# Six banks for an output projection, and a reordered start and end of the down products, in a fused decoder layer

## The chip, the cores and the metric

One core of a Trainium2 chip runs the whole layer as one program. The metric is the device time of one execution in microseconds. TensorE is called PE, VectorE DVE, ScalarE ACT, GpSimd POOL, and SyncE SP; SP issues most of the DMA transfers and POOL issues the stores of results.

## The reference

One inference step of a decoder layer (D = 1024) for a prompt of 1024 rows and a sample group of 64 rows (8 sequences of 8), which share the weights. The part that matters here is the end of the layer:

```python
    x = x + merged @ w_out
    f, conv_state = conv_ffn(rmsnorm(x, norm2_g), conv_prefix.astype(x.dtype), w_ffn_gate, w_ffn_up,
                             ffn_conv_w, ffn_conv_b, w_ffn_down)
    x = x + f
```

`conv_ffn` computes g = h @ w_gate and u = h @ w_up (1024 x 2816 each), a causal convolution of width 3 over the rows of g, then (gelu(gc) * u) @ w_down (2816 x 1024). After the layer comes a last `rmsnorm` of x with `final_norm_g`: each row is divided by the root of its mean square and multiplied by a gain per column.

## The kernel before

Everything is float32. A matmul runs on operands of a reduced format, so each operand is split into a high part (ACT casts it, L113) and a low part (DVE subtracts the high part from the source, L114), and a product is three matmuls: high x high, high x low and low x high. A matmul is 128 x 128 by 128 x 512; its result lies in one PSUM bank of 128 x 512.

The program is written in an order of its own, but a planner sets the order of the instructions on each engine: it takes the text's order as a priority, estimates durations, and puts an instruction ahead where its inputs and its buffer are free earlier. On the chip each engine and each DMA queue then works strictly in that order. Tiles with one tag turn through a fixed number of buffers.

The three places:

*Output projection (L944 to L1006).* For the two halves `nb` of 512 columns of `w_out`, the weights are loaded and split; then one product for the sample's rows and one for each of the eight row tiles t of the prompt (24 matmuls, L191). Each goes to a PSUM bank `nat`, of which there are two. `add_sq` (L928) adds the bank to x on DVE, in place, and squares the sum on ACT, writing the squares into the bank and their sum to `ssn`. In the second half x1 is stored to DRAM by a POOL DMA (L978), then normalised in place (`norm2`, L934 to L938: sum, a chain of small instructions for the reciprocal root at L120 to L126, one multiply over 1024 columns), transposed and split into the blocks B11, B21, B22 and T1 to T4 for the FFN products, which are computed by Winograd's scheme of seven products in place of eight. PSUM also has two tiles `big` of two banks each, which this stage doesn't use. The raw weights of the first two FFN blocks (L918) are loaded to buffers with the tag `raw`, of which there are four.

*FFN products (L1132).* Forty-four weight blocks, seven products each. The change does not touch their text.

*Down products (L1166 to L1481).* The product with `w_down` is also computed by Winograd's scheme, in seven passes in the order P1, P2, P5, P6, P7, P3, P4, each of 11 steps k. A step is twelve matmuls (four row tiles t, three each, L1298) to four banks of a ring of seven with tag `b`; P2 goes on adding into P1's banks and P7 into P6's. In P2, P6, P7 and P3 two more matmuls per step compute the sample's rows in a bank `sb` (L1338). `prep_down` loads and splits the operands of a step, four steps ahead of the matmuls, into five buffers `hd`. The first four operands come through `raw` buffers, the other seven of P1 through the tiles XB and ST, whose memory becomes free only after the FFN products. `sum1` and `sum2` turn ST into the sums that P5 and P6 use. After four steps the sample's own operand is made (L1390 to L1412): two transposes on PE, a multiply on DVE, casts on ACT and subtractions on DVE, and then the run goes on with step 4.

`evac` empties the banks after the last step of a pass: after P1 and P6 all four at once, after the others tile 0 at once and one more per step. Rows' squares are summed by `sq` (L1250), whose junk output goes to the bank just read. `norm` (L1252 to L1264) is the final norm: for row tiles 0 to 3 and the sample ACT multiplies by the reciprocal root (L1262), POOL by the gain (L1263) and POOL issues the store (L1264); for row tiles 4 to 7, which are finished at the end of P4, DVE does both in one instruction per half (L1259) and SP issues the stores. P4's last four steps are held back and computed tile by tile, so that the row tiles are finished one after another.

Of the kernel before, what the change touches and what calls it, by code (L numbers as in the profile page):

```python
# [16 lines left out]
P = 128  # L17
# [15 lines left out]
def hybrid_step(ctx, tc, x_prompt, x_sample, mem_prompt, cache_k, cache_v, page_table, state_pool,  # L33
# [888 lines left out]
    with tc.tile_pool(name="p5", bufs=1, reuse_waits="tile") as p5:  # L922
# [11 lines left out]
        def norm2(xt, n, t):  # L934
# [3 lines left out]
            nc.vector.scalar_tensor_tensor(xt, xt, r, g2b[:n], op0=ALU.mult, op1=ALU.mult)  # L938
# [14 lines left out]
        for nb in range(2):  # L953
            n0 = nb * 512
            wf = load_w(cols(w_out, n0))
            if nb == 0:
                nc.sync.dma_start(x1s, x_sample)
                for t in range(NT):
                    nc.sync.dma_start(x1[t], x_prompt[t * P:(t + 1) * P])
            else:  # L960
                nc.sync.dma_start(g2b, bc(norm2_g[0], P))
                raws[0], raws[1] = raw_ffn(0), raw_ffn(1)
            pt = nat()
# [8 lines left out]
            for i, t in enumerate((0, 2, 1, 3, 4, 6, 5, 7) if nb else range(NT)):  # L972
                pt = nat()
                mm_n(pt, wf, macts, t)
                add_sq(x1[t], (pt,), pt, P, t, nb)
                if nb == 0:
                    continue
                nc.gpsimd.dma_start(x1_d[t], x1[t])  # L978
                norm2(x1[t], P, t)
                if i == 3:  # L980
                    T1, T2 = [ap_.tile([P, 2, 4, 512], F32R, tag="act", bufs=4, name=f"T{q}") for q in (1, 2)]
                a = t // 2
                if t % 2 == 0:
                    put(B11, x1[t][:, 0:512], a)
                    put(B21, x1[t][:, 512:D], a)
                    continue
                xa, xb = x1[t - 1], x1[t]
                put(B22, xb[:, 512:D], a)
                nc.vector.tensor_tensor(xa[:, 0:512], xb[:, 0:512], xa[:, 0:512], op=ALU.subtract)
                nc.gpsimd.tensor_tensor(xb[:, 0:512], xb[:, 512:D], xb[:, 0:512], op=ALU.subtract)  # L990
                nc.vector.tensor_tensor(xb[:, 512:D], xb[:, 512:D], xa[:, 0:512], op=ALU.subtract)
                nc.gpsimd.tensor_tensor(xa[:, 512:D], xa[:, 512:D], xb[:, 512:D], op=ALU.subtract)
                todo.append((xa, xb, a))
                if T1 is not None:
                    for (xa, xb, a) in todo:
                        put(T1, xa[:, 0:512], a)
                        put(T2, xb[:, 512:D], a)
                        late.append((xa, xb, a))
                    todo = []
# [9 lines left out]
    with tc.tile_pool(name="fa", bufs=1, reuse_waits="tile") as fa:  # L1009
# [220 lines left out]
        def sum1(k):  # L1230
            ld(ST[k][:, 0], fA(1, 1, k))
            if k < 4:
# [4 lines left out]
        def sum2(k):  # L1237
            if k < 4:
# [9 lines left out]
        def sq(x, junk, i, c):  # L1248
            n = x.shape[0]
            nc.scalar.activation(junk, x, AF.Square, accum_out=ssf[:n, i, c:c + 1])  # L1250

        def norm(x, i, dst, late):  # L1252
            n = x.shape[0]
            ss = sm.tile([P, 1], F32, tag="ss", name=f"ss{uid()}")[:n]
            tt(ss, ssf[:n, i, 0:1], ssf[:n, i, 1:2], ALU.add)
            r = rstd_of(ss, n, 1.0 / D, 1)
            if late:
                for c in (LO, HI):
                    nc.vector.scalar_tensor_tensor(x[:, c], x[:, c], r, gfb[:n, c], op0=ALU.mult, op1=ALU.mult)  # L1259
                    nc.sync.dma_start(dst[:, c], x[:, c])  # L1260
            else:
                nc.scalar.activation(x, x, AF.Identity, scale=r)  # L1262
                nc.gpsimd.tensor_tensor(x, x, gfb[:n], op=ALU.mult)  # L1263
                nc.gpsimd.dma_start(dst, x)  # L1264

        def smp2(c, op):
            for h in range(2):
                tt(ys[:, c], ys[:, c], sb[0][h * TS:(h + 1) * TS], op)

        def evac(p, t, b):  # L1270
            y0, y1 = Y[t], Y[t + 4]
            if p == "P1":
                nc.scalar.copy(U[t], b)
            elif p == "P2":
                tt(y0[:, LO], y0[:, LO], b, ALU.add)
                sq(y0[:, LO], b, t, 0)
            elif p == "P5":
                tt(y0[:, HI], b, U[t], ALU.subtract)
                nc.scalar.copy(y1[:, HI], b)
            elif p == "P6":  # L1280
                tt(y0[:, HI], y0[:, HI], b, ALU.subtract)
            elif p == "P7":
                tt(U[t], U[t], b, ALU.add)
                tt(y1[:, HI], y1[:, HI], U[t], ALU.subtract)
                sq(y1[:, HI], b, t + 4, 1)
                tt(y1[:, LO], y1[:, LO], U[t], ALU.add)
            elif p == "P3":
                tt(y0[:, HI], y0[:, HI], b, ALU.add)
                sq(y0[:, HI], b, t, 1)
                norm(y0, t, y_prompt[t * P:(t + 1) * P], False)  # L1290
            else:
                tt(y1[:, LO], y1[:, LO], b, ALU.add)
                sq(y1[:, LO], b, t + 4, 0)
                norm(y1, t + 4, y_prompt[(t + 4) * P:(t + 5) * P], True)
# [6 lines left out]

        def run_steps(s0, s1):
            for g in range(4, s0 + 4 if s0 else 0):
                prep_down(g)
            for s in range(s0, s1):
# [3 lines left out]
                if s >= 4:  # L1309
# [13 lines left out]
                    if pend:  # L1323
                        evac(*pend.pop(0))
# [17 lines left out]
                now = 4 if p in ("P1", "P6") else 1  # L1342
                for t in range(4):
                    if t < now:
                        evac(p, t, banks[t])
                    else:
                        pend.append((p, t, banks[t]))
                if p == "P6":
                    smp2(LO, ALU.add)
                if p == "P7":  # L1350
                    smp2(LO, ALU.subtract)
                    smp2(HI, ALU.add)
                    sq(ys[:, LO], sb[0][0:TS], NT, 0)
                if p == "P3":
                    smp2(HI, ALU.add)
                    sq(ys[:, HI], sb[0][0:TS], NT, 1)
                    norm(ys, NT, y_sample, False)
            if s1 == len(steps):
                for t in range(4):
                    for (k, h) in held:  # L1360
                        mm4("P4", k, t, h)
                    evac("P4", t, banks[t])
# [27 lines left out]
        run_steps(0, 4)  # L1390
# [25 lines left out]
    with tc.tile_pool(name="fb", bufs=1, reuse_waits="tile") as fb:  # L1416
        XB, ST = {}, {}
        for k in (4, 5, 6, 7, 8, 9, 10, 0, 1, 2, 3):
            XB[k] = fb.tile([P, 2, 512], F32, name=f"XB{k}")
            ST[k] = fb.tile([P, 2, 512], F32, name=f"ST{k}")  # L1420
        ssf = fb.tile([P, NT + 1, 2], F32, name="ssf")
        run_steps(4, len(steps))
# [59 lines left out]
```

## Time and profile before

| | us |
|---|---|
| median of 3 runs | 1769.6 (1768.57 to 1771.12) |
| the profiled execution | 1768.74 |
| its span from the first to the last instruction | 1767.0 |
| PE busy | 1698.4 (96%) |
| DVE busy | 952.8 (54%) |
| ACT busy | 723.2 (41%) |
| POOL busy | 412.1 (23%) |
| mean granted clock of PE, of 1 | 0.986 |

PE is busy for nearly the whole span, and the chain of waits that ended last runs on PE for 84% of it. A busy PE is not PE at its peak: a matmul takes about twice as long at the lower of the two clocks (1.2 GHz, shown as 0.50; 2.4 GHz is 1.00). So a stretch is read by its idle time and by the granted clock together.

### The profile page before, as it was taken

Reading aid. Unit: us, or ns where it says so; the run is one execution under the profiler, and the core shown is the slowest. Engines: PE = TensorE matmul, PEld = TensorE weight load, DVE = VectorE, ACT = ScalarE, POOL = GpSimd, SP = SyncE. Lnnn points to the kernel's source line nnn. Section 1 sums busy time; section 2 is a strip of 40 time slices with the busy share of each in tenths; the row PEclk is TensorE's granted clock in tenths of the full one; section 3 lists DMA queues with packets and bytes.
Section 4 is the critical chain, followed back from the end, with each engine's and each line's share of the span. In section 5 each row is a group of like instructions: output and inputs, shape, how many; then the busy total and the mean of one; then the engine's idle time right before and its main releaser. Section 6 shows DMA issues by size and latency. Waiting matters only on the chain.

```text
span 1767.0 us, 22904 instructions
## 1 busy us (share of the span) xinstructions
PE 1698.4 (96%) x8157; PEld 1327.8 (75%) x8157; DVE 952.8 (54%) x1648; ACT 723.2 (41%) x1397; POOL 412.1 (23%) x438
## 2 busy tenths in 40 slices
PE   7999999999999999999989899999999999899996
PEld 5887876765666787777768778888888888688875
DVE  6412134330220766676734776666666666578778
ACT  5422234331330766665522354444444444344343
POOL 1113020300200324202200244444444442100003
PEclk9999999999999999999999999999999999999998
DMA  7432251357665424154542132222222222891513
GB/s 272 152 131 82 79 171 59 110 180 237 201 223 193 136 86 142 34 167 155 182 167 66 72 63 72 73 73 73 73 73 72 73 73 84 299 337 49 177 68 137
DMA packets 142359, 228.18 MB, mean 129 GB/s; under 512 B 26703, under 2 KB 64109, under 8 KB 142245
## 3 DMA queue, kind: packets, MB, share of 16 engines
q1 hardware_dynamic: 126453, 178.25, 31.3%
q0 software_dynamic: 15792, 48.48, 8.1%
q8 instruction: 64, 1.05, 0.2%
q14 instruction: 50, 0.41, 0.1%
HBM read 176.19 MB, written 50.54 MB: 128 GB/s over the span
## 4 chain that ended last, share of the span: by engine, by line
PE 84%; DVE 6%; DMA 3%; issue 3%; ACT 2%; SPq 1%; POOL 1%; DVEq 0%; POOLq 0%; ACTq 0%
PE nat L182 18%; PE big L1132 17%; PE P L1298 10%; PE nat L191 8%; PE nat L1132 7%; PE big L182 4%; PE tp L110 4%; PE av L1047 3%; PE big L781 2%; PE av L811 2%; PE nat L199 2%; PE av L110 1%; PE av L571 1%; PE sb L1338 1%; PE big L675 1%
## 5 line engine op out<-in xcount | busy, mean ns | idle before, releaser
L182 PE MATMUL nat<-act,hl 128*128 128x512 f32 x1344 | 359.3, 405 | 0.0
L182 PEld LDWEIGHTS nat<-act,hl 128*128 128x128 f32 x1344 | 242.7, 189 | 62.1 <-issue 15.1
L1298 PE MATMUL P<-hd 128*128 128x512 f32 x924 | 223.7, 397 | 12.9 <-ACT hd L113 6.1
L1298 PEld LDWEIGHTS P<-hd 128*128 128x128 f32 x924 | 176.7, 192 | 52.5 <-ACT hd L113 6.7
L191 PE MATMUL nat<-hl,act 128*128 128x512 f32 x768 | 187.6, 402 | 6.8 <-ACT nat L932 5.1
L191 PEld LDWEIGHTS nat<-hl,act 128*128 128x128 f32 x768 | 146.9, 193 | 39.0 <-ACT nat L932 5.5
L1132 PE MATMUL big<-B,wA 128*128 128x512 f32 x528 | 131.2, 396 | 0.0
L114 DVE TENSOR_TENSOR hl<-raw,hl 128x1024 fp32r<-128x1024 f32 x52 | 66.4, 1288 | 117.1 <-ACT hl L113 115.8
L1132 PEld LDWEIGHTS big<-B,wA 128*128 128x128 f32 x528 | 95.9, 188 | 24.4 <-ACT gu L1157 6.3
L114 DVE TENSOR_TENSOR wB<-stm,wB 128x512 fp32r<-128x512 f32 x44 | 50.7, 1154 | 102.1 <-ACT wB L113 102.1
L474 POOL DMA_DIRECT2D gl<-ev x48 | 26.2, 547 | 280.8 <-ACT ev L473 256.5
L473 ACT COPY ev<-nat 128x512 f32<-128x512 f32 x48 | 28.1, 586 | 116.1 <-PE nat L182 115.6
L1115 POOL TENSOR_TENSOR stm<-rf,stm 128x512 f32<-128x512 f32 x22 | 28.7, 1304 | 188.3 <-DVE wB L114 188.2
L1132 PE MATMUL nat<-B,wC 128*128 128x512 f32 x264 | 70.5, 389 | 0.0
L113 ACT CAST hl<-raw 128x1024 fp32r<-128x1024 f32 x60 | 62.5, 1051 | 16.8 <-PE nat L182 7.9
L1132 PE MATMUL big<-T,wC 128*128 128x512 f32 x264 | 66.4, 400 | 0.0
L114 DVE TENSOR_TENSOR hd<-rd,hd 128x1024 fp32r<-128x1024 f32 x37 | 49.3, 1334 | 30.2 <-ACT hd L113 25.9
L1132 PE MATMUL nat<-T,wB 128*128 128x512 f32 x264 | 64.9, 394 | 0.0
L1132 PE MATMUL big<-T,wD 128*128 128x512 f32 x264 | 64.0, 391 | 0.0
L113 ACT CAST hd<-rd 128x1024 fp32r<-128x1024 f32 x37 | 38.9, 1051 | 60.1 <-PE sb L1338 31.9
L1132 PE MATMUL big<-T,wB 128*128 128x512 f32 x264 | 63.4, 389 | 0.0
L1148 DVE TENSOR_TENSOR gu<-gu,big 128x512 f32<-128x512 f32 x44 | 30.3, 688 | 57.2 <-PE big L1132 57.2
(450 smaller groups left out, 3168.8 us busy)
## 6 DMA issues: line engine op xcount, KB each, us to landing
raw<-in_w_in SPq DMA_DIRECT2D x40, 512.0 KB
kr<-in_cache_k SPq DMA_DIRECT2D x64, 256.0 KB
vr<-in_cache_v SPq DMA_DIRECT2D x64, 256.0 KB
rd<-f_d SPq DMA_DIRECT2D x59, 256.0 KB
gl<-ev POOLq DMA_DIRECT2D x48, 256.0 KB, 2.7
rd<-in_w_ffn_down SPq DMA_DIRECT2D x48, 256.0 KB
rf<-in_w_ffn_gate SPq DMA_DIRECT2D x22, 512.0 KB
rf<-in_w_ffn_up SPq DMA_DIRECT2D x22, 512.0 KB
```

The lines of the kernel that those rows point to most:

```text
L110: nc.tensor.transpose(out, in_, ident[:n, :n])
L113: nc.scalar.copy(hi, src)
L114: (lo_eng or nc.vector).tensor_tensor(lo, src, hi.bitcast(F32), op=ALU.subtract)
L182: nc.tensor.matmul(out, wf(k, pw)[:, n0:n0 + P], acts[c][ph][:, k, :], start=(k == ks[0] and (pw, ph) == (0, 0)), stop=(k == ks[-1] and (p ...
L191: nc.tensor.matmul(out, acts[c][ph][:, k, o:o + P], wf(k, pw), start=(k == ks[0] and (pw, ph) == (0, 0)), stop=(k == ks[-1] and (pw, ph) = ...
L199: nc.tensor.matmul(out, stack[:, k, :], wf(k, pw), start=(k == ks[0] and pw == 0), stop=(k == ks[-1] and pw == 1))
L781: nc.tensor.matmul(S[:, k0:k0 + n], Qd[:, m, part, qs], Kst[:, m, k0:k0 + n], start=(part == 0), stop=(part == 1))
L811: nc.tensor.matmul(av[:, :P], aT[:, k * P:(k + 1) * P], vn[:, k0 + k], start=(k0 + k == 0), stop=(k0 + k == i))
L1047: nc.tensor.matmul(pt[:, i * 256:(i + 1) * 256].rearrange("p (h x) -> p h x", h=2), xs[:, k] if k < 4 else st2[:, k - 4], w[n1][:, :, k] i ...
L1132: nc.tensor.matmul(out, wt[:, pw, k], Bt[:, ph, k], start=(start and k == 0 and (pw, ph) == (0, 0)), stop=(k == 3 and (pw, ph) == (1, 0)), ...
L1148: nc.vector.tensor_tensor(hv(g, i), hv(g, i), q(x), op=ALU.add)
L1298: nc.tensor.matmul(banks[t], h[:, ph, 0, t * P:(t + 1) * P], h[:, pw, 1], start=(k == 0 and p not in ("P2", "P7") and (pw, ph) == (0, 0)), ...
```

## The change

1. *Banks of the projection.* `obank` gives the nine products of the first half six banks: two `nat` and the four halves of the two `big` tiles. The second half keeps the two `nat`.
2. *x1 in halves.* In the first half the lower 512 columns of x1 are stored as soon as they are added. In the second half `add_sq` writes the sum to a stage (`stg`: two `raw` buffers, four halves) in place of x1; the store reads the stage, and `norm2` multiplies the two halves in two instructions. Only the first FFN block is loaded ahead; the second follows where the FFN products begin.
3. *Start of the down products.* Step 4's operand also comes through a `raw` buffer and is prepared ahead of step 0; after step 0 the sample's operand is made, and then the run goes on with step 1. XB[4] and ST[4] are filled later, by `sum1` and `sum2`.
4. *Reading the banks.* `evac` is a generator: each of its pieces is one or two instructions, and `more(n)` runs n pieces at a step. In P7 the first piece adds bank 0 into U, all squares take bank 3 for junk, and the sample's adds come between.
5. *The final norm.* The reciprocal root for row tiles 0 to 3 is one chain on four columns; DVE multiplies by root and gain in one instruction of 1024 columns per tile, also for the sample, and POOL only issues the stores. The upper halves of row tiles 4 to 7 are multiplied by the gain ahead of time. `last` takes the place of `norm` at the end of P4: one instruction of the chain fewer, the upper half scaled on ACT, the lower on DVE.

```diff
-        def add_sq(xt, pts, junk, n, t, nb):
+        def add_sq(xt, pts, junk, n, t, nb, out=None):
             xh = xt[:, nb * 512:(nb + 1) * 512]
+            out = xh if out is None else out
             for q in pts:
-                nc.vector.tensor_tensor(xh, xh, q, op=ALU.add)
-            nc.scalar.activation(junk, xh, AF.Square, accum_out=ssn[:n, t, nb:nb + 1])
+                nc.vector.tensor_tensor(out, xh, q, op=ALU.add)
+            nc.scalar.activation(junk, out, AF.Square, accum_out=ssn[:n, t, nb:nb + 1])
...
+            for (c, src) in ((slice(0, 512), xt[:, 0:512]), (slice(512, D), hi)):
+                nc.vector.scalar_tensor_tensor(xt[:, c], src, r, g2b[:n, c], op0=ALU.mult, op1=ALU.mult)
+
+        obs, obc = [], [0]
+
+        def obank(nb):
+            obc[0] += 1
+            if nb or obc[0] % 6 in (1, 2):
+                return nat()
+            if not obs:
+                pt = big()
+                obs.extend((pt[:, 0], pt[:, 1]))
+            return obs.pop(0)
...
-                raws[0], raws[1] = raw_ffn(0), raw_ffn(1)
-            pt = nat()
+                raws[0] = raw_ffn(0)
+                stg = [wp.tile([P, 2, 512], F32, tag="raw", bufs=4, name=f"stg{i}") for i in range(2)]
+            pt = obank(nb)
...
-                add_sq(x1[t], (pt,), pt, P, t, nb)
                 if nb == 0:
+                    add_sq(x1[t], (pt,), pt, P, t, nb)
+                    nc.gpsimd.dma_start(x1_d[t][:, 0:512], x1[t][:, 0:512])
                     continue
-                nc.gpsimd.dma_start(x1_d[t], x1[t])
-                norm2(x1[t], P, t)
+                hi = stg[i % 4 // 2][:, i % 2]
+                add_sq(x1[t], (pt,), pt, P, t, nb, hi)
+                nc.gpsimd.dma_start(x1_d[t][:, 512:D], hi)
+                norm2(x1[t], P, t, hi)
...
-                if k < 4:
+                if k < 5:
                     src = rawt(fA(0, 0, k), wB(0, 0, k))
...
+        def norm(xs_, i, dsts):
+            n, w = xs_[0].shape[0], len(xs_)
+            ss = sm.tile([P, w], F32, tag=f"rs_s{w}", bufs=1, name=f"ss{uid()}")[:n]
+            tt(ss, ssf[:n, 0, i:i + w], ssf[:n, 1, i:i + w], ALU.add)
+            r = rstd_of(ss, n, 1.0 / D, w)
+            for j, (x, dst) in enumerate(zip(xs_, dsts)):
+                def go(x=x, dst=dst, j=j):
+                    nc.vector.scalar_tensor_tensor(x, x, r[:, j:j + 1], gfb[:n], op0=ALU.mult, op1=ALU.mult)
+                    nc.gpsimd.dma_start(dst, x)
+                yield go
+
+        def last(t, b):
+            y, i = Y[t + 4], t + 4
+            dst = y_prompt[i * P:(i + 1) * P]
+            tt(y[:, LO], y[:, LO], b, ALU.add)
+            sq(y[:, LO], b, i, 0)
...
+            nc.vector.tensor_scalar(a, ssf[:, 0, i:i + 1], 1.0 / D, ssf[:, 1, i:i + 1], op0=ALU.mult, op1=ALU.add)
+            nc.scalar.activation(q, a, AF.Sqrt)
...
+            nc.scalar.activation(y[:, HI], y[:, HI], AF.Identity, scale=r)
+            nc.sync.dma_start(dst[:, HI], y[:, HI])
+            nc.vector.scalar_tensor_tensor(y[:, LO], y[:, LO], r, gfb[:, LO], op0=ALU.mult, op1=ALU.mult)
+            nc.sync.dma_start(dst[:, LO], y[:, LO])
...
             elif p == "P7":
-                tt(U[t], U[t], b, ALU.add)
-                tt(y1[:, HI], y1[:, HI], U[t], ALU.subtract)
-                sq(y1[:, HI], b, t + 4, 1)
-                tt(y1[:, LO], y1[:, LO], U[t], ALU.add)
+                yield lambda: tt(U[0], U[0], bk[0], A)
+                for h in range(2):
+                    yield lambda h=h: smp1(LO, S, h, sbk)
+                    yield lambda h=h: smp1(HI, A, h, sbk)
+                for t in range(1, 4):
+                    yield lambda t=t: tt(U[t], U[t], bk[t], A)
+                for t in range(4):
+                    yield lambda t=t: tt(Y[t + 4][:, HI], Y[t + 4][:, HI], U[t], S)
+                    yield lambda t=t: (sq(Y[t + 4][:, HI], bk[3], t + 4, 1), tt(Y[t + 4][:, LO], Y[t + 4][:, LO], U[t], A))
+                sq(ys[:, LO], bk[3][0:TS], NT, 0)
             elif p == "P3":
...
+                yield from norm([Y[t] for t in range(4)], 0, [y_prompt[t * P:(t + 1) * P] for t in range(4)])
+                for t in range(4):
+                    yield lambda t=t: tt(Y[t + 4][:, HI], Y[t + 4][:, HI], gfb[:, HI], ALU.mult)
+                nc.vector.tensor_scalar(ssf[:, 1, 4:8], ssf[:, 1, 4:8], 1.0 / D, EPS, op0=ALU.mult, op1=A)
+                yield from norm([ys], NT, [y_sample])
...
-                    if pend:
-                        evac(*pend.pop(0))
+                    more(4 if k == 0 else 1 if p != "P3" and p != "P4" or k > 6 else 2)
...
-        run_steps(0, 4)
+        prep_down(4)
+        run_steps(0, 1)
...
-        for k in (4, 5, 6, 7, 8, 9, 10, 0, 1, 2, 3):
+        for k in (5, 6, 7, 8, 9, 10, 0, 1, 2, 3, 4):
...
-        run_steps(4, len(steps))
+        run_steps(1, len(steps))
```

## Rows read from the trace of the kernel before

**Rows 1.** Windows of time: stretch, its length, busy us of each engine (instructions), clock, DMA share, GB/s.
```profile
897.00:949.00 52.00, 46.89 (x195) 38.20 (x194) 11.23 (x15) 9.28 (x20) 0.00 (x0) 0.93 0.34 120
1046.00:1506.00 460.00, 460.00 (x2163) 372.72 (x2162) 286.94 (x367) 197.67 (x356) 180.32 (x158) 1.00 0.24 74
1506.00:1546.00 40.00, 33.96 (x142) 26.98 (x141) 21.95 (x26) 14.91 (x24) 6.22 (x6) 0.91 0.93 316
...
1719.70:1757.70 38.00, 32.98 (x133) 25.87 (x131) 33.96 (x73) 19.23 (x34) 17.21 (x10) 0.91 0.38 132
```

**Rows 2.** Chain of waits, in P5 and P6: start, us, what.
```profile
1580.97 32.64 PE P L1298 x144
```

**Rows 3.** Timeline of the projection's start: start, us, engine, what [idle before <- releaser].
```profile
897.44 5.64 PE L191 MATMUL nat<-hl,act 128*128 128x512 f32 x24
...
905.84 1.40 DVE L931 TENSOR_TENSOR x1s<-x1s,nat 64x512 f32<-64x512 f32 x2 [5.55 <-DMA x1s<-in_x_sample]
...
908.19 41.16 PE L191 MATMUL nat<-hl,act 128*128 128x512 f32 x168 [5.11 <-ACT nat L932]
```

**Rows 4.** Groups of DVE instructions, 955 to 1033: busy us, mean ns, idle before.
```profile
L938 DVE SCALAR_TENSOR_TENSOR x<-x,rsy,g2b 128x1024 f32<-128x1024 f32 x8 | 10.3, 1285 | 3.9 <-DMA x_d<-x 3.7
...
L126 DVE TENSOR_TENSOR rsy<-rsy,rst 128x1 f32<-128x1 f32 x8 | 1.3, 160 | 0.3
```

**Rows 5.** Waits in the second half: total us, times, longest.
```profile
DVE x L938 <- DMA x_d<-x: 3.7, 4, 1.3
...
PE av L110 <- DVE x L938: 2.9, 1, 2.9
```

**Rows 6.** Timeline where the FFN products begin.
```profile
1028.70 1.69 SPq L1023 DMA_DIRECT2D cwb<-in_ffn_conv_b  x1
...
1029.42 1.14 ACT L113 CAST wA<-rf 128x512 fp32r<-128x512 f32 x2
```

**Rows 7.** Timeline of the start of the down products.
```profile
1518.33 0.34 PE L110 MATMUL sb<-ident,gs 64*128 64x64 f32 x2
...
1523.79 0.61 ACT L113 CAST hd<-XB 128x512 fp32r<-128x512 f32 x1
...
1524.97 23.81 PE L1298 MATMUL P<-hd 128*128 128x512 f32 x96 [5.57 <-ACT hd L113]
...
1531.13 0.62 ACT L113 CAST hd<-XB 128x512 fp32r<-128x512 f32 x1 [1.44 <-DMA XB<-f_d]
```

**Rows 8.** Timeline of P7 to P3.
```profile
1682.65 1.28 DVE L1197 TENSOR_TENSOR uy<-uy,P 128x512 f32<-128x512 f32 x2
...
1685.34 6.86 PE L1298 MATMUL P<-hd 128*128 128x512 f32 x22 [2.32 <-ACT P L1250]
```

**Rows 9.** Timeline of P4.
```profile
1719.69 20.11 PE L1298 MATMUL P<-hd 128*128 128x512 f32 x88
...
1742.62 4.50 DVE L114 TENSOR_TENSOR hd<-rd,hd 128x1024 fp32r<-128x1024 f32 x2
...
1746.04 11.64 PE L1298 MATMUL P<-hd 128*128 128x512 f32 x41 [4.34 <-DVE hd L114]
```

**Rows 10.** Groups of DVE and POOL instructions, 1719 to 1747.
```profile
L114 DVE TENSOR_TENSOR hd<-rd,hd 128x1024 fp32r<-128x1024 f32 x8 | 11.8, 1484 | 0.0
L1197 DVE TENSOR_TENSOR rd<-rd,ST 128x512 f32<-128x512 f32 x5 | 5.6, 1116 | 0.0
L126 DVE TENSOR_TENSOR rsy<-rsy,rst 128x1 f32<-128x1 f32 x4 | 4.9, 1214 | 0.0
L126 DVE TENSOR_TENSOR rsy<-rsy,rst 64x1 f32<-64x1 f32 x1 | 2.2, 2160 | 0.0
...
L1263 POOL TENSOR_TENSOR yy<-yy,uy 128x1024 f32<-128x1024 f32 x4 | 11.5, 2894 | 205.5 <-ACT rst L121 205.1 <-ACT yy L1262 0.4
...
L1264 POOL DMA_DIRECT2D out<-yy x4 | 2.3, 585 | 0.6 <-POOL yy L1263 0.6
```

**Rows 11.** Timeline of the end.
```profile
1762.30 1.41 DVE L1259 SCALAR_TENSOR_TENSOR yy<-yy,rsy,uy 128x512 f32<-128x512 f32 x2
```

More of the change, by code (lines that the diff above doesn't have):

```diff
@@ L1249, in sq @@
             n = x.shape[0]
[L1250 to L1271, printed above, removed]
+            nc.scalar.activation(junk, x, AF.Square, accum_out=ssf[:n, c, i:i + 1])
+        def norm(xs_, i, dsts):
[8 more added lines that the diff above has]
+                yield go
@@ L1272, in evac, with smp1 @@
+        def smp1(c, op, h, b):
+            tt(ys[:, c], ys[:, c], b[h * TS:(h + 1) * TS], op)
+        def evac(p, bk, sbk):
+            A, S = ALU.add, ALU.subtract
             if p == "P1":
-                nc.scalar.copy(U[t], b)
+                for t in range(4):
+                    nc.scalar.copy(U[t], bk[t])
             elif p == "P2":
-                tt(y0[:, LO], y0[:, LO], b, ALU.add)
-                sq(y0[:, LO], b, t, 0)
+                for t in range(4):
+                    yield lambda t=t: tt(Y[t][:, LO], Y[t][:, LO], bk[t], A)
+                    sq(Y[t][:, LO], bk[t], t, 0)
@@ L1277, in evac @@
             elif p == "P5":
-                tt(y0[:, HI], b, U[t], ALU.subtract)
-                nc.scalar.copy(y1[:, HI], b)
+                for t in range(4):
+                    yield lambda t=t: (tt(Y[t][:, HI], bk[t], U[t], S), nc.scalar.copy(Y[t + 4][:, HI], bk[t]))
             elif p == "P6":
-                tt(y0[:, HI], y0[:, HI], b, ALU.subtract)
+                for t in range(4):
+                    tt(Y[t][:, HI], Y[t][:, HI], bk[t], S)
+                for h in range(2):
+                    yield lambda h=h: smp1(LO, A, h, sbk)
@@ new lines, in evac @@
+                for h in range(2):
+                    yield lambda h=h: smp1(LO, S, h, sbk)
+                    yield lambda h=h: smp1(HI, A, h, sbk)
+                for t in range(1, 4):
+                    yield lambda t=t: tt(U[t], U[t], bk[t], A)
+                for t in range(4):
+                    yield lambda t=t: tt(Y[t + 4][:, HI], Y[t + 4][:, HI], U[t], S)
+                    yield lambda t=t: (sq(Y[t + 4][:, HI], bk[3], t + 4, 1), tt(Y[t + 4][:, LO], Y[t + 4][:, LO], U[t], A))
@@ L1300, in mm4, with more @@
                                  stop=(k == KH - 1 and (pw, ph) == (1, 0)), skip_group_check=True)
+        def more(n):
+            while n and pend:
+                f = next(pend[0], None)
+                if f is None:
+                    pend.pop(0)
+                    continue
+                f()
+                n -= 1
         def run_steps(s0, s1):
-            for g in range(4, s0 + 4 if s0 else 0):
-                prep_down(g)
             for s in range(s0, s1):
@@ L1341, in run_steps @@
                     continue
[L1342 to L1357, printed above, removed]
+                pend.append(evac(p, list(banks), sb[0]))
+                more(1)
             if s1 == len(steps):
@@ L1361, in run_steps @@
                         mm4("P4", k, t, h)
-                    evac("P4", t, banks[t])
+                    if t == 0:
+                        more(99)
+                    last(t, banks[t])
         S1AT = {4 + (13 * k) // 10: k for k in range(KH)}
```

35 lines of the change are left out of this document (22 added, 13 removed).

## The prediction

> **What bounds the kernel now.** I read the table of busy time by window first. Between 1046 and 1506 us TensorE (PE) has no idle time [rows 1], and the change touches nothing there: the 460 us of FFN products stay as they are. Idle PE, and PE at a lower granted clock, stand around the places that the change edits: 897 to 949 (46.89 busy of 52, clock 0.93), 1506 to 1546 (33.96 of 40, clock 0.91) and 1719.7 to 1757.7 (32.98 of 38, clock 0.91) [rows 1]. Then I took waits and timeline of each of these. Each time PE waits for one operand or one bank and then runs its next matmuls more slowly, so a stall is paid twice. The price of a matmul at full clock is from the chain of waits, where 144 take 32.64 us: 0.2267 each [rows 2], 5.44 for a projection tile of 24, 2.72 for a down step of 12.
>
> **The change part by part.** The sum is made against the profiled execution (1768.74 us, span 1767.0).
>
> *A, six banks in the first half of the output projection.* Now two nat banks turn. The sample's add waits for its x1s load (DVE idle 5.55 us until 905.84), its square lets go of the bank on ACT, and PE, which had ended the first tile at 903.08 (897.44 + 5.64), goes on at 908.19 after 5.11 us of idling [rows 3]. The 168 matmuls behind it take 41.16 us instead of 168 x 0.2267 = 38.08: 3.08 us go to the clock. With six banks tiles 1 to 4 go to the halves of the two big tiles, which nothing else uses in this half, and a nat bank is wanted again only after five tiles of 5.44 us, at 924.8. A = 5.11 + 3.08 = 8.2 us. Late next could be the x loads of the other adds, behind x1s on SP; now the add of the first tile follows at once behind that of the sample, and 16 us of cover are left. Bounds: 5.1 (the clock stays low for another reason) to 8.2.
>
> *B, x1 written in halves, the upper one from a stage.* In the second half the normalisation can't overwrite x1 before its store is read: four waits, 3.7 us on DVE [rows 5]. They go. One multiply of 1285 ns [rows 4] becomes two halves, at 0.64 to 0.7 each: at most +0.1 us for each of eight tiles. The eight extra stores are issued on POOL in the first half, where it has nothing to do [rows 1]. PE waits for that multiply 2.9 us at the end [rows 5]; the last tile's multiply starts with the end of its root chain and not with its store, so most of this stays. The stage takes two of the four raw buffers, so the second FFN weight block is loaded only when the stage is free. I take B = 1.0 us; ends: +3 (DVE's waits and PE's all gone), and -6, if these loads come behind the conv loads: the last of those holds SP's queue until 1030.4 (1028.70 + 1.69), and a load of some 4 us would then land about 5 us after the first split of that block at 1029.42 [rows 6].
>
> *C, the first down step alone, then the sample's operand; five steps split ahead.* Now PE runs four steps, then the sample's two transposes at 1518.33, and its next product starts at 1524.97 [rows 7]. Step 4's operand is not late by DMA: its cast starts at 1523.79 with no idle ahead of it [rows 7], right behind the sample's casts on ACT. From 1518.40 (the end of step 3) that is 6.57 us. Behind it 96 matmuls take 23.81 instead of 21.76: 2.05 us of clock. Afterwards the transposes stand behind step 0, about 1510, and cost 0.34 and 0.3 of PE with some 0.35 of wait for DVE between them: 0.95. The sample's casts lie beside steps 1 to 4 (10.9 us), and step 4's operand comes through a raw buffer, ahead of them. So 6.57 + 2.05 - 0.95 = 7.7, if the next operands follow. Late next is DMA: in 1506 to 1546 it is busy 0.93 of the time [rows 1], and the operand cast at 1531.13, step 9's, waited for its load [rows 7]. With one pair of loads less ahead, step 10's takes that place; it is wanted at 1510.9 + 9 x 2.72 = 1535.4 and split about 2 us after 1531.13. The margin is 2 us here and no larger in the first steps of P2. I take C = 7.0, between 7.7 and 2 (DMA yields only that much).
>
> *D, bank reads spread at P7 to P3.* The fourth bank of P3 is P7's first; it is let go by a square on ACT that uses it as junk, behind add and subtract. PE idles 2.32 us until 1685.34, and 22 matmuls then take 6.86 instead of 4.99 [rows 8]: 4.19 us. After the change the add into U alone frees that bank; in DVE's present order it starts at 1682.65 and takes 0.64 [rows 8], so PE would wait from 1683.02 to about 1683.35. D = 3.8, from 0 (if DVE meets a wait for P4's loads first) to 4.2.
>
> *E, four norms in one chain, no POOL.* In P4 the last four operands are needed together. PE ends 88 matmuls at 1739.80 and starts the last 41 at 1746.04, 11.64 us long, so it ends at 1757.68 [rows 9]; 132 at full clock would end at 1749.6: 8.1 us are lost. DVE is late, and it is slowed while POOL multiplies (2.9 us each): the last step of the root chain takes 1214 and 2160 ns there [rows 10] and 160 elsewhere [rows 4], a subtraction 1116 instead of 640, a split 1484 [rows 10] against 1285 for the multiply of its size. Together 4 x 1.05 + 2.0 + 5 x 0.47 + 8 x 0.2 = 10.2 us. These go. Of five root chains three go, 21 small instructions, of which DVE's own time is about half: 1.5 us. Added on DVE: five full multiplies at 1.285, 6.4 us, and four half ones, 2.6, which I expect in DVE's idle time in P3. So DVE's last split ends 2.7 to 5.3 us sooner than 1747.12 [rows 9], at 1743 or so; it is wanted at 1719.69 + 93 x 0.2267 = 1740.8. PE still idles some 2.5 us and loses near 2 us of clock, 4.5 to 5 of the 8.1. I take E = 3.0; ends: 8.1 (no stall) and -2 (if the single chain, which waits for all four squares, puts its multiplies ahead of the last splits and they end later than now).
>
> *F, the end.* From PE's end to DVE's last multiply are 6.0 us (1763.71), 3.3 more to the end of the span [rows 11]. The chain of the last tile now stands behind two multiplies of the tile before (1.41, as the pair of rows 11), one of its adds goes, and half of the last multiply goes to ACT: add 0.7, square 0.8, chain 1.6, half multiply 0.7 = 3.8, and 0.3 for a second store issued behind the first. F = 9.3 - 3.8 - 3.3 - 0.3 = 1.9, from 1 to 2.3.
>
> Sum: 8.2 + 1.0 + 7.0 + 3.8 + 3.0 + 1.9 = 24.9. 1768.74 - 24.9 = 1743.8; the median of the runs shown is 1769.6, 0.9 above the profiled one, so **1744.7**.
>
> POOL still issues the output stores while DVE has more to do than before. Beside a DVE that is never idle such an issue took 585 ns here, four times [rows 10]. The Trainium skill, SBUF — State Buffer, "A bandwidth-pool intuition that's wrong", says that an issue can wait for a port that DVE holds, and gives about 3100 ns instead of 620. By that page five issues would take 15 us of POOL, by the row 2.9; either way they lie ahead of the last tile's stores, which SP issues, and the sum stays. For this mix of DVE work the trace disagrees with the page.
>
> **The rivals.**
> 1. *The down steps become DMA-bound.* For: 0.93 DMA share and a margin of 2 us. Against: one pair of loads less ahead of step 10. C falls to 2: 1749.7.
> 2. *P4 stays bound by DVE.* The chain for four rows and the sample's own norm stand in DVE's order before the split of step 10. For: 6.4 us of new multiplies. Against: 10.2 us of blocking gone. E = -2: 1749.7.
> 3. *The second FFN weight block is late*, behind the conv loads on SP. B = -6 and 1 us of clock: 1752.7. Against: its buffers come free before the conv loads' memory does.
> 4. *The six banks don't do what they say*, because the order on PE still puts something that waits for x1s ahead: A = 0, 1752.9. Against: PE's first tile runs beside that wait today.
> 5. *Slower.* A load of the down steps at the head of SP's queue waits for a raw buffer that only PE's progress frees, and all XB and ST loads stand behind it. DMA has only 0.07 of 1506 to 1546 to spare [rows 1], so each us that it idles there is a us of PE, and gaps halve the clock: over the 17 steps from step 5 to the end of P2 half clock is 17 x 2.72 = 46 us more. The sign turns when DMA stops for about 10 us and PE runs over a third of these steps at half clock; with half of them it is 1744.7 + 10 + 23 = 1778. Against: at half clock PE asks for less, and the loads catch up.
>
> **How the numbers follow.** The forecast with all terms near their values: 0.56. Rival 1: 0.13, rival 2: 0.12, rival 3: 0.07, rival 4: 0.05, slower: 0.07. The forecast alone reaches from 1736 (C, D, E, B and F at their best ends take off 0.7, 0.4, 5.1, 2 and 0.4) to 1749; the rivals 1 to 4, one or two of them together, up to 1757. Range 1736 to 1757; it leaves out rival 5 and about as much of the others. A measurement here can't tell less than 0.2%, 3.5 us, from no change: faster 0.91, same 0.03 (three rivals at once, or a part of rival 5), slower 0.06.
>
> **What would show it.** A: no idle PE between 903 and 908, clock 1.00 there. C: step 0's matmuls, then the transposes, then unbroken P1 at full clock; waits of PE for hd show rival 1. D: less than 0.6 us of idling in P3's first step. E: no POOL multiply after P3; the last split some 23 us after P4's start, with a PE gap of 2 to 3 us. F: 7.3 to 7.5 us from PE's last matmul to the end. The prediction is wrong if the stage of FFN products changes length, or if PE gets new waits in P1 and P2 of more than 5 us.

## The result

The changed kernel takes 1748.09 us (median of four, 1747.25 to 1752.75) against 1770.36 beside it: a ratio of 0.9873 [0.9858, 0.9889], 22 us less. Forecast were 1744.7, in a range of 1736 to 1757. The direction and the range held; the sum of 24.9 us was 2.6 too large, and inside it two terms were far off, in opposite directions.

The profiled execution of the changed kernel is the longest of its four (1752.75, span 1751.0; before 1767.0). Up to 894 us, where the two kernels are the same, it is already 2.45 us behind. First the windows of time, with the columns of [rows 1]; the last one is now the stretch of P4, which ends sooner:

```profile
897.00:949.00 52.00, 51.60 (x226) 41.78 (x225) 17.99 (x22) 12.31 (x25) 5.27 (x9) 1.00 0.51 178
1046.00:1506.00 460.00, 460.00 (x2156) 371.90 (x2154) 286.36 (x361) 194.90 (x352) 183.62 (x160) 1.00 0.25 74
1506.00:1546.00 40.00, 35.10 (x147) 28.23 (x148) 22.82 (x27) 15.72 (x24) 2.51 (x4) 0.96 0.93 313
1712.40:1743.10 30.70, 30.42 (x133) 24.51 (x132) 27.19 (x56) 15.11 (x29) 2.71 (x5) 1.00 0.47 165
```

PE is full in the projection and in P4, where it had 46.89 of 52 and 32.98 of 38; the FFN products have not moved. But 1506 to 1546 has gained one microsecond of work only. PE's timeline (start, us, engine, what, idle before and releaser) shows where the old waits were, at the projection, the start of the down products, P7 to P3 and P4:

```profile
899.89 5.64 PE L191 MATMUL nat<-hl,act 128*128 128x512 f32 x24
905.37 16.73 PE L191 MATMUL big<-hl,act 128*128 128x512 f32 x72
...
1508.27 0.27 PE L110 MATMUL sb<-ident,gc 128*44 128x128 f32 x1 [1.16 <-DVE fsv L1081]
1508.30 10.47 PE L1349 MATMUL P<-hd 128*128 128x512 f32 x45
1522.51 20.97 PE L1349 MATMUL P<-hd 128*128 128x512 f32 x84 [3.74 <-ACT hd L113]
...
1675.64 5.20 PE L1349 MATMUL P<-hd 128*128 128x512 f32 x21
1682.17 0.70 PE L1395 MATMUL sb<-hd,fsy 128*128 128x512 f32 x2 [1.32 <-DVE uy L1217]
...
1712.44 21.69 PE L1349 MATMUL P<-hd 128*128 128x512 f32 x95
1734.33 8.69 PE L1349 MATMUL P<-hd 128*128 128x512 f32 x37 [0.20 <-DVE hd L114]
```

The wait of 5.11 us behind the first projection tile [rows 3] is gone, and so are those of 2.32 [rows 8] and 4.34 [rows 9]. Two waits are new: 3.74 us for step 5's operand in place of 5.57 for step 4's [rows 7], and 1.32 us for the sample's bank. The wait of 1.16 us at the transposition of gc (the last rows of the convolution) was 0.47 before. The terms in the two profiled executions, each the change of the distance between two matmuls that both kernels have (us saved). In the kernel before P5's first matmul is taken at 1580.80, where PE's timeline has it, as in the kernel after; the chain of waits [rows 2] counts it from 1580.97:

| term | from, to | forecast | measured |
|---|---|---|---|
| A | first projection tile to the second half: 51.74, 44.06 | 8.2 | 7.7 |
| B | second half to the first product big<-T,wB: 83.70, 84.68 | 1.0 | -1.0 |
| C | first matmul of P1 to that of P5: 73.74, 72.82 | 7.0 | 0.9 |
| D | P5 to P4: 138.89, 136.55 | 3.8 | 2.3 |
| E | first to last matmul of P4: 37.99, 30.58 | 3.0 | 7.4 |
| F | last matmul to the end of the span: 9.32, 7.98 | 1.9 | 1.3 |

They sum to 18.7; less the 2.45 of the start and 0.26 of the FFN products that is 16.0, the difference of the spans. So the questions were: where did C's 6 us go, is B a loss, and what did the prediction miss in E?

ACT's and SP's timelines of the changed kernel show what step 5 waits for:

```profile
1509.19 2.51 SPq L1207 DMA_DIRECT2D yy<-x_d  x4
1511.80 1.41 SPq L1207 DMA_DIRECT2D uy<-x1s_d  x1
1513.26 0.58 SPq L1207 DMA_DIRECT2D uy<-in_final_norm_g  x1
1513.99 0.32 SPq L1207 DMA_DIRECT2D XB<-f_d  x1
```

```profile
1512.78 0.24 ACT L113 CAST fsz<-fsv 128x64 fp32r<-128x64 f32 x1
1521.23 0.62 ACT L113 CAST hd<-XB 128x512 fp32r<-128x512 f32 x1 [8.22 <-DMA XB<-f_d]
```

ACT is done with the sample's operand at 1513.0 and then idles 8.22 us for a load that was issued at 1513.99 and let ACT go on 7.2 us later. Ahead of it SP had issued 1.75 MB that nobody wants before P2's end: four halves of Y, the sample's x1 and the last norm's gain. In SP's order they stand right ahead of step 5's load. They stood so in the kernel before, ahead of step 4's:

```profile
1509.90 2.07 SPq L1187 DMA_DIRECT2D yy<-x_d  x4
...
1513.29 0.54 SPq L1187 DMA_DIRECT2D XB<-f_d  x1
```

### The profile page after: what moved, and what is told of

The parts are those of the page before. It is cut to its first block, busy times and chain, and to the rows that moved or that the text cites. A ratio compares the mean times of both kernels' runs of the same rounds, so it can differ in the third digit from the quotient of the medians.

```text
span 1751.0 us, 22916 instructions
## 1 busy us (share of the span) xinstructions
PE 1697.0 (97%) x8157; PEld 1324.6 (76%) x8157; DVE 948.9 (54%) x1636; ACT 720.1 (41%) x1392; POOL 401.0 (23%) x441
## 4 chain that ended last, share of the span: by engine, by line
PE 84%; DVE 6%; DMA 4%; ACT 2%; issue 2%; POOL 1%; SPq 1%; ACTq 0%; POOLq 0%; DVEq 0%
PE nat L182 18%; PE big L1152 18%; PE nat L191 8%; PE P L1349 8%; PE nat L1152 7%; PE big L182 4%; PE tp L110 4%; PE av L1067 3%; PE nat L199 2%; PE av L811 2%; PE big L781 2%; PE av L110 2%; PE big L191 2%; DMA rd<-f_d 1%; PE av L571 1%
## 5 line engine op out<-in xcount | busy, mean ns | idle before, releaser
L191 PE MATMUL nat<-hl,act 128*128 128x512 f32 x648 | 157.5, 398 | 1.7 <-DVE act L114 1.0
L191 PEld LDWEIGHTS nat<-hl,act 128*128 128x128 f32 x648 | 121.9, 191 | 28.0 <-DVE act L114 1.8
```

The source lines that it names most:

```text
L191: nc.tensor.matmul(out, acts[c][ph][:, k, o:o + P], wf(k, pw), start=(k == ks[0] and (pw, ph) == (0, 0)), stop=(k == ks[-1] and (pw, ph) = ...
```

## The experiments

Each kernel was timed beside the kernel before; the ratios are to that one, with their intervals.

**The changed kernel again** (no edit).

> The changed kernel once more, unaltered. Theory 1 (order of the loads): four loads for Y, the sample's x and the last norm's weight, 1.75 MB, stand ahead of step 5's operand in SP's order in every execution, so a new profile shows TensorE idle near 3.7 us again between steps 4 and 5 of the first down block, and the fifth product starts at the same distance (72.8 us) from the end of the gate/up blocks as in the profiled run; time 1748 +- 1. Rival: that execution was a long one (its total was 4 us over the other three), the wait is mostly its own, and a new profile shows under 1.5 us of it with a span near 1746.

1750.31 us (1747.52 to 1752.46), 0.9873 [0.9858, 0.9888]. The profiled execution, at 1752.46, shows the wait again:

```profile
1507.62 10.47 PE L1349 MATMUL P<-hd 128*128 128x512 f32 x45
1521.86 22.10 PE L1349 MATMUL P<-hd 128*128 128x512 f32 x84 [3.77 <-ACT hd L113]
```

P1 to P5 takes 73.6 us. Theory 1 held on the wait; the time lies above its 1748 +- 1. But both profiles are of long executions.

**Output projection on two banks.**

```
-            if nb or obc[0] % 6 in (1, 2):
+            if True:
                 return nat()
```

> Output projection back on its two banks, everything else of the change kept. Theory (the bank read is what held the products, term A of the prediction, seen as 7.7 us in the two profiles): 1755.8, 7 to 8.5 us slower than the changed kernel. Rival (the vector additions of the second half's x1 and the norm behind them were the bound, the staging and the half stores brought the gain): within 1 us of the changed kernel, 1748 to 1749.

1756.37 us (1752.89 to 1757.63), 0.9913 [0.9899, 0.9926]: 6.1 over the run of the changed kernel beside it.

```profile
896.88 5.61 PE L191 MATMUL nat<-hl,act 128*128 128x512 f32 x24
908.29 40.36 PE L191 MATMUL nat<-hl,act 128*128 128x512 f32 x168 [5.80 <-ACT nat L933]
948.48 1.75 PE L199 MATMUL nat<-hl,ms 128*128 128x512 f32 x7
```

The wait of [rows 3] is back, and the stretch is 51.6 us against 44.06 with six banks: 7.5, as the theory says. The time of 6.1 more is a little under its 7 to 8.5. The bank read is what held PE. In this profile the wait for step 5's operand is 2.23 us, and P1 to P5 takes 69.7.

**Old start of the down products, then late loads, then both.** The old start undoes part 3 of the change alone: four steps are split ahead and run, and then the sample's operand is made. The late loads are held back by a write of one element, which has to wait for the landing of step 10's operand:

```
+   nc.gpsimd.tensor_copy(Y[s - 8][:, 0:1], XB[10][:, 0, 0:1])
    ld(Y[s - 8][:, LO], x1_d[s - 8][:, LO])
...
+   nc.gpsimd.tensor_copy(ys[:, 0:1], XB[10][:TS, 0, 0:1])
    ld(ys, x1s_d)
+   nc.gpsimd.tensor_copy(gfb[:, 0:1], XB[10][:, 0, 0:1])
    ld(gfb, bc(final_norm_g, P))
```

> Four steps split ahead and the sample's operand after them, as in the kernel before; the rest of the change kept. Theory 1 (the new order only moved the wait to step 5's load, as the two profiles show): 1749 to 1750, 1 to 2 us slower than the changed kernel. Rival (the wait at step 5 belongs to the one profiled run, and the part is worth what was forecast, 7.0): 1754 to 1755.5.

> The loads of Y's first four halves, the sample's x and the last norm's weight are made to follow the landing of step 10's operand (one element of each target is first written from it by GpSimd), so that step 5's operand is the first load after step 4's. Theory 1 (order of the loads): TensorE's idle before step 5 goes from 3.7 to under 1 us and the low clock behind it goes, 1742.5 to 1745. Rival 2 (the transfers as a whole bound the first block, any order): the wait comes back at a later step, 1747 to 1749. Rival 3 (GpSimd's writes and SP's waits hold the loads of the sums up): above 1749.

> Four steps split ahead and the sample's operand behind them, as in the kernel before, with the late loads of the run before (Y, sample's x and last weight follow step 10's landing); the rest of the change kept. Theory 1 (the order of the loads was the whole wait, in the kernel before as in the changed one): step 4's operand lands some 6 us sooner, the 5.6 us wait of TensorE before step 4 falls under 1 us, and the time is within 1.5 us of the late-loads kernel, 1745 to 1747. Rival (the fifth step split ahead is needed, since the buffers of the loads come free only behind the sample's operand): a wait of 2.5 to 4 us stays, with the low clock behind it 1749 to 1751.

| | loads early | loads late |
|---|---|---|
| old start | 1752.87, 0.9894 [0.9879, 0.9909], P1 to P5 73.5 us | 1751.89, 0.9886 [0.9868, 0.9903], 73.3 us |
| new start | 1750.31, 0.9873 [0.9858, 0.9888], 73.6 us (72.8 and 70.4 in the two other profiles of this kernel) | 1745.30, 0.9848 [0.9835, 0.9862], 67.0 us |

Timed once more, the new start with late loads gave 1745.24, 0.9836 [0.9822, 0.9849], with 66.8 us:

> The late-loads kernel once more, as the one to compare with on the same chip: 0.985 of the kernel before, no wait of TensorE for step 5's operand in the profile.

Against the upper left cell the late loads alone move the stretch by 0.2 us and the new start alone by -0.2 to 0.6 in its long executions and by 3.1 in a short one (below); both together shorten it by 6.4 to 6.7. The time of the old start, 2.6 over the changed kernel beside it, lies between its theory and its rival. With both edits, PE has 129 matmuls without a gap, and the cast of step 5 starts 11.3 us after P1's first matmul (1501.28) instead of 18.2 (1521.23 - 1503.07). Its load is issued 6.1 us after that matmul (1507.38) instead of 10.9, and ACT goes on 5.2 us later instead of 7.2, so 4.8 us were SP's queue and 2.0 the transfer:

```profile
1506.47 0.27 PE L110 MATMUL sb<-ident,gc 128*44 128x128 f32 x1 [1.15 <-DVE fsv L1081]
1506.49 29.52 PE L1349 MATMUL P<-hd 128*128 128x512 f32 x129
```

```profile
1510.98 0.24 ACT L113 CAST fsz<-fsv 128x64 fp32r<-128x64 f32 x1
1512.57 0.62 ACT L113 CAST hd<-XB 128x512 fp32r<-128x512 f32 x1 [1.35 <-DMA XB<-f_d]
```

That is theory 1 of the late loads; the times are 0.2 to 0.3 above its band. Rival 2 (the transfers as a whole are the bound) did not occur in these two profiles: the DMA share was 1.02 in 1508 to 1520 of the first, and no step came late. But it is near. In the profiles of the next two kernels below (GpSimd's multiplication, four chains), which have the same start and the same late loads, PE waits 2.0 and 1.8 us for operands in P2, in three pieces each, and P1 to P5 takes 70.1 and 69.8. The largest piece:

```profile
1552.13 1.20 PE L1350 MATMUL P<-hd 128*128 128x512 f32 x4 [0.97 <-ACT hd L113]
```

For the combination of old start and late loads my theory 1 fell. The loads were issued from 1502.88 on, step 4's operand lay ready, and the wait was 5.56 us, as with the loads early:

```profile
1511.69 1.36 ACT L113 CAST fsy<-fsv 128x1408 fp32r<-128x1408 f32 x1 [10.88 <-DVE fsv L1081]
1512.96 0.26 ACT L1447 COPY ncv<-sb 44x128 f32<-44x128 f32 x1
1515.67 0.73 ACT L113 CAST fsy<-fsv 128x640 fp32r<-128x640 f32 x1 [2.45 <-DVE fsv L1461]
1516.30 0.24 ACT L113 CAST fsz<-fsv 128x64 fp32r<-128x64 f32 x1
1516.45 0.61 ACT L113 CAST hd<-XB 128x512 fp32r<-128x512 f32 x1
```

```profile
1517.63 23.65 PE L1349 MATMUL P<-hd 128*128 128x512 f32 x96 [5.56 <-ACT hd L113]
```

There the cast follows the sample's operand on ACT without a pause, as the prediction read it from [rows 7]. It is not quite the rival either, which spoke of buffers: it is ACT's order. Two things of nearly equal length stood side by side, and in the long executions each hid the other.

**The changed kernel a third time** (no edit).

> The changed kernel a third time, for one more profile. Its executions so far fall in two groups, 1747.3 to 1748.6 and 1752.0 to 1752.8 us, and both profiles are of the upper one. Theory (the wait for step 5's load and the low clock behind it make the difference): a time under 1749 goes with a first block, from its first matmul to that of the fifth product, of under 71 us, a time over 1751.5 with 73 or more. Rival (the difference comes from the part ahead of the gate/up blocks): 73 or more in either case.

1748.61 us, and P1 to P5 takes 70.35 us:

```profile
1506.68 10.47 PE L1349 MATMUL P<-hd 128*128 128x512 f32 x45
1519.58 19.35 PE L1349 MATMUL P<-hd 128*128 128x512 f32 x84 [2.43 <-ACT hd L113]
```

The wait is 1.3 us shorter, and the 84 matmuls behind it are not slowed. That is 3.3 us of the 3.9 between this execution and the one at 1752.46: the theory held. So C is 3.4 in a short execution of the changed kernel and 0.1 to 0.9 in a long one.

**One chain, with GpSimd's multiplication back; and four chains without it** (both with late loads).

```
-   nc.vector.scalar_tensor_tensor(x, x, r[:, j:j + 1], gfb[:n], op0=ALU.mult, op1=ALU.mult)
+   nc.scalar.activation(x, x, AF.Identity, scale=r[:, j:j + 1])
+   nc.gpsimd.tensor_tensor(x, x, gfb[:n], op=ALU.mult)
```

> Late loads kept; the four norms of the first Y tiles stay in one chain but go back to a scaling on ScalarE and a multiplication by the weight on GpSimd. Theory 1 (GpSimd's multiplication and stores held VectorE's small steps and the splits up in the fourth product): the stretch from the first matmul of the fourth product to the last goes from 30.6 to 36 or more, time 1751 to 1753. Rival (the single chain and its place ahead of the splits brought it): the stretch stays under 32.5, time under 1747.5.

```
-   yield from norm([Y[t] for t in range(4)], 0, [y_prompt[t * P:(t + 1) * P] for t in range(4)])
+   for t in range(4):
+       yield from norm([Y[t]], t, [y_prompt[t * P:(t + 1) * P]])
```

> Late loads kept; VectorE's one-pass multiplication kept; the four norms get a chain of small steps each instead of one for all. Theory 1 (GpSimd was the cost, the chain is worth little): 24 more small steps of 0.16 us, 3.9 us of VectorE that TensorE's 30.4 us cover, the stretch stays under 31.5, time 1745 to 1746.5. Rival (the chain is what the prediction priced): the stretch grows by 3 us or more, 1748 and above.

With the multiplication: 1753.60 us, 0.9889 [0.9869, 0.9908], and P4 takes 36.4 us, 5.8 more than with the late loads alone. With four chains: 1747.37 us, 0.9856 [0.9838, 0.9873], and P4 takes 30.6, as with one. Both theories held on P4; the times are 0.6 and 0.9 over their bands. Both profiled executions are the longest of their four: besides the waits in P2 above they were 2.3 and 3.9 us behind the late loads' profile before the projection began. DVE's groups of instructions in P4 (busy, mean ns, idle), first of the changed kernel, then with GpSimd's multiplication, and GpSimd's own groups there:

```profile
L114 DVE TENSOR_TENSOR hd<-rd,hd 128x1024 fp32r<-128x1024 f32 x7 | 8.5, 1218 | 0.0
L1217 DVE TENSOR_TENSOR yy<-yy,P 128x512 f32<-128x512 f32 x6 | 3.9, 680 | 0.8 <-PE P L1349 0.8
L1217 DVE TENSOR_TENSOR rd<-rd,ST 128x512 f32<-128x512 f32 x5 | 3.3, 681 | 0.0
```

```profile
L114 DVE TENSOR_TENSOR hd<-rd,hd 128x1024 fp32r<-128x1024 f32 x7 | 15.2, 2181 | 0.0
L1217 DVE TENSOR_TENSOR rd<-rd,ST 128x512 f32<-128x512 f32 x5 | 5.5, 1126 | 0.9 <-DMA rd<-in_w_ffn_down 0.9
L1217 DVE TENSOR_TENSOR yy<-yy,P 128x512 f32<-128x512 f32 x7 | 4.6, 684 | 2.1 <-PE P L1350 2.1
...
L1280 POOL TENSOR_TENSOR yy<-yy,uy 128x1024 f32<-128x1024 f32 x4 | 10.1, 2536 | 194.6 <-ACT yy L1279 194.6
```

The seven splits cost 6.7 us more and the five subtractions 2.2. It is three of the splits, at 3.43 to 3.44 us, and one subtraction, at 2.88, that stand beside a multiplication:

```profile
1720.74 2.51 POOL L1280 TENSOR_TENSOR yy<-yy,uy 128x1024 f32<-128x1024 f32 x1 [194.58 <-ACT yy L1279]
1720.90 3.43 DVE L114 TENSOR_TENSOR hd<-rd,hd 128x1024 fp32r<-128x1024 f32 x1
```

Without a multiplication beside it the last split of the changed kernel is this one:

```profile
1733.06 1.21 DVE L114 TENSOR_TENSOR hd<-rd,hd 128x1024 fp32r<-128x1024 f32 x1
```

The addition that reads one of its inputs from PSUM costs the same in both, but only one of the seven stood beside a GpSimd multiplication (1737.09, 0.69 us). More telling are the 44 additions gu<-gu,big of the FFN products: all take 686 to 689 ns, those beside a GpSimd instruction with two SBUF inputs included (1057.84 beside 1057.12 to 1058.42).

**x1 whole again** (with late loads and six banks): one store of 1024 columns, `norm2` in place, the second weight group loaded ahead.

```
...
-   hi = stg[i % 4 // 2][:, i % 2]
-   add_sq(x1[t], (pt,), pt, P, t, nb, hi)
-   nc.gpsimd.dma_start(x1_d[t][:, 512:D], hi)
-   norm2(x1[t], P, t, hi)
+   add_sq(x1[t], (pt,), pt, P, t, nb)
+   nc.gpsimd.dma_start(x1_d[t], x1[t])
+   norm2(x1[t], P, t)
```

> Late loads and six banks kept; the output projection's second half goes back to x1 itself, one store of 1024 columns, one norm pass, and the second weight group loaded ahead. Theory 1 (the halves lost 0.9 us, as the two profiles show): from the first matmul of the projection's second half to the first product of the gate/up blocks 59.2 us instead of 60.0, time 1744 to 1745.5. Rival (the forecast: halves bring 1 us): 61 us, time 1746 to 1747.

1745.16 us, 0.9845 [0.9828, 0.9862]: the same as with halves. From the second half's first matmul to the first product are 58.6 us against 60.0, a little more than theory 1 said, but to big<-T,wB it is 84.0 against 84.2 and 83.2 in the two profiles of the late loads: the next products give it back. The time lies in theory 1's band, but it is no better than the late loads' own; no gain of either form shows. DVE's groups of this kernel, then of the late loads:

```profile
L940 DVE SCALAR_TENSOR_TENSOR x<-x,rsy,g2b 128x1024 f32<-128x1024 f32 x8 | 10.3, 1284 | 3.3 <-DMA x_d<-x 3.2
```

```profile
L943 DVE SCALAR_TENSOR_TENSOR x<-x,rsy,g2b 128x512 f32<-128x512 f32 x8 | 6.0, 752 | 0.3
L943 DVE SCALAR_TENSOR_TENSOR x<-stg,rsy,g2b 128x512 f32<-128x512 f32 x8 | 6.0, 745 | 0.0
```

With halves the 3.2 us of waiting for the stores go, 1.7 us of longer multiplies come, and the waits of the root chains for ACT grow from 3.4 + 1.7 to 4.5 + 2.5.

**The two small new waits** (with late loads). In the first kernel P3's first two sample matmuls are issued with those of the second step, in the second also the transposition of gc ahead of step 0.

```
+   hold.append((k, h))
+   if p == "P3" and k == 0:
+       continue
+   for (kk, hh) in hold: ...
```

> Late loads kept; the sample's two matmuls of the sixth product's first step (P3-0) are issued together with those of its second step. Theory 1 (term D lost 1.3 us to them, since their bank waits for the sample's four additions): the 1.3 us wait of TensorE is gone, the seventh product starts 1.3 us sooner after the fifth, 1 to 1.5 us faster than the late-loads kernel. Rival (VectorE's queue of additions is late as a whole): the wait comes back at a split of the next steps or at the fourth bank, gain under 0.4 us.

> The kernel of the run before, and the transposition of the last convolution rows (gc) goes ahead of the first down step instead of behind the sample's operand, whose bank it waited for. Theory 1 (TensorE's 1.15 us wait there was on the bank alone): another 1.1 us, in sum 2 to 2.6 us faster than the late-loads kernel, about 1743. Rival (step 5's operand, which has some 2.5 us in hand, or the sample's operand becomes late): the wait moves, in sum under 1.5 us.

1746.49, 0.9840 [0.9827, 0.9854], and 1745.58, 0.9837 [0.9824, 0.9851], beside 1745.24 for the late loads alone: no gain, where the theories promised 1 to 1.5 and 2 to 2.6 us. The planner put the four sample matmuls only three main matmuls later, and the wait went from 1.28 to 0.63 us:

```profile
1672.27 3.71 PE L1349 MATMUL P<-hd 128*128 128x512 f32 x15 [0.44 <-DVE uy L1217]
1676.61 1.17 PE L1402 MATMUL sb<-hd,fsy 128*128 128x512 f32 x4 [0.63 <-DVE uy L1217]
```

P5 to P4 is 136.3 us against 136.5 and 137.0 in the two profiles without the edit. That fits the rival, that DVE's queue is late there as a whole. The wait of 1.15 us at the transposition is gone in the second kernel, and PE's last matmul comes 233.7 us after P1's first, against 234.2 and 234.4: 0.5 us, less than the runs tell apart. The best version measured is the changed kernel with the late loads, 0.984 to 0.985 of the kernel before.

## Why the prediction was right, and where it was wrong

- **A was right** in mechanism and size: 7.7 of 8.2, and undoing it alone costs 7.5 in its stretch and 6.1 in time. Rival 4 is out. The sample's add still waits 5.93 us for its load. But the cover is less than the 16 us that the prediction counted: in four later profiles of this stage PE waits 0.62 to 0.77 us, 31 matmuls into the big banks, for a square on ACT. Why a big bank waits so early I have not followed.
- **B failed** in "they go. [...] at most +0.1 us for each of eight tiles": two halves cost 1.50 us against 1.28, twice what I allowed, and the chain was also held by ACT's squares. The -1.0 of the table is no steady loss: the same stretch took 83.15 to 84.76 us in the later profiles with halves, against 83.70 before and 84.01 with x1 whole. No gain can be told from 0. Rival 3 did not occur.
- **C failed** in one step: "The margin is 2 us here". I priced the loads as if only their number counted and looked for the first late one at step 10; it was step 5's. The first half, that the sample's operand on ACT held step 4, is shown by the old start with late loads. But the loads' order on SP was a second hold of nearly the same length right behind it: 1.75 MB of early loads ahead of step 5's. The order was in the trace of before, where nothing waited for it; I read who released the cast and not when its load had been issued (1513.29, behind the same loads). Rival 1 named the right resource at the wrong place and for the wrong reason: the same bytes in another order cost nothing in P1, and up to 2.0 us in P2 in two of the profiles with late loads. Its sign, waits of PE for hd, came.
- **D was half right**: the wait for the fourth bank went, but I asked only who else reads that bank, not what is pushed back in DVE's order. The sample's four adds now stand among the adds into U and hold the sample's bank: 1.32 us of idling, where the sign was less than 0.6. That the order of these adds alone is the cause is not shown.
- **E was undersized**: 7.4 for 3.0. The blocking was priced about right: against [rows 10] the splits and the subtractions lost 2.1 and 2.2 us, and the last steps of the root chains the 6.2 that I counted, 10.5 for 10.2. GpSimd's multiplication brings 8.9 us of blocking back, then on splits and a subtraction. The failed step is the last: "at 1743 or so", 23.3 us after P4's start, where 21.1 were wanted. I took the middle of 2.7 to 5.3, whose worse end charged the four half multiplies to P4, though I expected them in P3. They ran in P3 (ended by 1696.9), and the last split ended 21.8 us after P4's start, 5.6 sooner than before. PE waited 0.20 us in place of the 2 to 3 forecast. An error of 1.5 us in DVE's work thus became 4.4 in PE's time, because the idling and the low clock behind it went together. By the Trainium skill, SBUF — State Buffer, "Who interferes with whom", a DVE instruction with two SBUF inputs contends with a GpSimd instruction that reads SBUF, and one with at most one SBUF input, outside the two-port modes, does not. The rows above agree: a split goes from 1.22 to 3.43 us, an addition with one input in PSUM stays at 0.69. The same section infers that a tensor_tensor leaves the issue of stores alone; the five issues in P4 took 540 to 552 ns here, beside a DVE without idle time. So the prediction was wrong to say that the trace disagrees with the page: the 3100 ns that it took from the Trainium skill stand there for a DVE tensor_copy, and P4 has none.
- **F**: 1.3 of 1.9; from PE's last matmul to the end are 7.98 us, where 7.3 to 7.5 were forecast. The last tile's root on ACT stands behind the upper half of the tile before (1744.72, 0.71 us; the root starts at 1745.33, its input was there at 1745.06). That accounts for 0.27; the rest I have not followed.

The forecast came within 3.4 us because E's surplus of 4.4 paid for part of what the other terms missed (10.6 in the profiled executions, 2.5 less in the short one profiled). That was luck.

## What to carry to other kernels

When a wait is removed, look at what else would have been late at the same moment: compare the landing of the next operand's load with the time at which it will now be wanted, and read the queue's order behind it, not its mean share. A load that nobody needs for a long time should be made to depend on the loads that are urgent; free buffers and an idle queue are enough to let it go first. And an elementwise operation given to GpSimd to unload DVE is to be charged at what it adds to DVE's instructions with two SBUF inputs.

## What the runs showed of the hardware

A wait's price is not its length alone. Behind 2.43 us of idling 84 matmuls took 19.35 us, near the 19.0 of [rows 2]'s price; behind 3.74 and 3.77 us they took 20.97 and 22.10. But behind 2.32 us, in P3 of the kernel before, 22 matmuls took 6.86 instead of 4.99 [rows 8], and the granted clock was 0.75 over 1685.3 to 1692. In the execution with 3.77 us it was 0.66 over 1520 to 1530, and 1.00 in the same window of the third execution:

```profile
1520.00:1530.00 10.00, 8.14 (x24) 6.48 (x25) 8.26 (x12) 5.96 (x10) 0.00 (x0) 0.66 1.04 400
```

```profile
1520.00:1530.00 10.00, 10.00 (x46) 8.24 (x45) 8.82 (x13) 6.33 (x11) 0.00 (x0) 1.00 1.05 397
```

The changed kernel's executions fall into two groups, 1747.3 to 1748.6 and 1752.0 to 1752.8 us, 4 us apart, and with the late loads alone they lie within 1743.5 to 1746.9. In the three that were profiled the group goes with this wait; for the others that is not shown. One GpSimd multiplication of 2.5 us stretched a single split on DVE from 1.22 to 3.43 us (the two lines at 1720.74 and 1720.90 above).
